# A decoder trunk on one core: an order planned with slack on VectorE and ScalarE, and three small steps on all partitions

## The chip, the cores and the metric

The kernel runs on one core of a Trainium2 chip. The core has five engines that run their own instruction queues side by side: TensorE (PE; its weight loads are shown as PEld), VectorE (DVE), ScalarE (ACT), GpSimd (POOL) and SyncE (SP), which here issues the transfers. The metric is the device time of one execution in microseconds (us). Times of a kernel are given as the median of several runs.

## The reference

The kernel computes a trunk of two layers on 256 tokens of width 1024, in float32. Cut to what matters:

```python
for l in range(DEPTH):                                   # 2
    h = _rms_norm(x, g_pre_mix[l])
    nq, kc, vc, ksel, vsel, kwin, vwin, gates, fq, fk, fv, ff = jnp.split(h @ w_in[l], ...)
    o_nsa = _nsa_mixer(...)     # 8 heads, 2 key/value groups: compressed, selected and window attention, gated
    o_fox = _fox_mixer(...)     # 8 heads
    mix = jnp.concatenate([o_nsa, o_fox], axis=-1) @ w_out[l]
    x = x + _rms_norm(mix, g_post_mix[l])
    h = _rms_norm(x, g_pre_mlp[l])
    y = jnp.square(jax.nn.relu(h @ w_up[l])) @ w_down[l]
    x = x + _rms_norm(y, g_post_mlp[l])
```

Two parts matter for the change. The compressed branch turns overlapping blocks of 32 keys (and values) into one key (value) each, by a small network with a bias at its end:

```python
hid = jax.nn.gelu(blocks @ w1 + b1)
return hid @ w2 + b2                                     # block keys, block values
```

The forgetting attention (`_fox_mixer`) adds differences of running sums of the log forget gates to its scores:

```python
log_f = jax.nn.log_sigmoid(f_logits + f_bias)
cum = jnp.cumsum(log_f, axis=1)
logits = q @ k.T * scale + cum[q] - cum[k]
```

## The kernel before

**Products.** Most matrix products run in TensorE's rounded float32 type. To keep float32 accuracy each operand is split in a rounded high part (`whi` for weights, written by ScalarE from the loaded chunk `wraw`) and a low part (`wlo`, VectorE: `wraw` minus `whi`), and three products are made: high by high, high by low, low by high. So every chunk of weights, 128 x 1024, needs one transfer, one ScalarE and one VectorE instruction. Transpositions are products with an identity (`cst`, `identr`).

**Stages of a layer.** Norm and input projections; rotation of queries and keys; the block network and the block keys and values; compressed, selected and window attention (NSA) and forgetting attention (FoX), whose score tiles `s` and `x` are exponentiated with VectorE and ScalarE (`pr`, row statistics `st`), transposed (`prT`, `prX`) and multiplied by the values into `o`; output projection of `oT`; MLP in eight chunks up and down. During attention, products of later projections (`acc<-xT,whi`, `acc<-whi,xT`, and behind them `x<-whi,oT`, `acc<-whi,oT`) are put between the attention's own products as fillers.

**What sets the order.** The program isn't emitted as it is written. A `Recorder` takes down every operation with its engine, a key for its rank, and a modelled duration (`op.cost = _cost(op, views)` in `add`). `schedule` then plays the program through as a list scheduler: on each engine it starts the ready operation that ranks first, with modelled costs, fixed latencies between engines (`_latency`) and the counts of free buffers; a load is taken to have ended 2900 ns after its bytes are through. `deadlines` derives due times from the order so found, `order` repeats this up to four times (PASSES) and keeps the plan that ends first. `emit` issues all in that order (this is the line L397 which most instructions of the profile carry). So a change of a modelled cost moves instructions of all engines, in the entire program. The cost of a VectorE instruction is

```python
return 68 + 64 * aps + n * (0.52 if fast else 1.04) + 10 * (op.name == "tensor_tensor_reduce")
```

in ns, with `n` columns and `aps` operands that are one value per partition; ScalarE's is `n / 1.2` plus 55 or 92, plus 93 for each such operand. The number of partitions doesn't enter.

**The three steps that are edited.** A tile has 128 partitions.
- `compressed_k` writes block keys into `kbd`, block-diagonal over two halves of 64 partitions: two VectorE instructions on 64 partitions each add the bias to the product's result; the other blocks stay zero from a memset at the program's start.
- `compressed_v` does the same for block values: one instruction on 128 partitions writes `vt` (result plus bias), then for each half of the partitions one copies it rounded into `vrep` (high part) and one subtracts (low part). `compressed_vT` transposes `vrep` on TensorE (tile `s<-identr,vrep`).
- `forget_sums` makes the running sums by two products into `s`. ScalarE copies them rounded into `cum`, in two pieces (128 and 256 columns); on partitions 32 to 63 and 96 to 127 VectorE replaces the copy by the low part, result minus copy, with two instructions for each of these two quarters. Products with `selr` add them to the scores (`s<-cum,selr`).

They are called once per layer, `compressed_k` directly and the others from a dictionary of steps that run beside the attention heads.

Of the kernel before, what the change touches and what calls it, by code (L numbers as in the profile page):

```python
# [18 lines left out]
F32 = mybir.dt.float32  # L19
F32R = mybir.dt.float32r  # L20
AF = mybir.ActivationFunctionType
# [3 lines left out]
P = 128  # L25
# [9 lines left out]
LANE = 0.9  # L35
PASSES = 4
LANDING = 2500.0
WAIT = 0.7
WARM = 4
ENTER, LEAVE = 90, 200  # L40
# [12 lines left out]
SEGS = ((0, 128, 0), (128, 384, 1))  # L53
GELU_C = 1.5957691216057308

C_ID, C_ROPE, C_SID, C_TRI, C_MASK, C_CM, C_M01, C_SEL, C_END = np.cumsum(
    [0, 128, 64, 32, 256, 256, 32, 32, 16]).tolist()


def constants():  # L60
    c = np.zeros((P, C_END), np.float32)
    i = np.arange(P)
    c[:, C_ID:C_ID + P] = np.eye(P)
    causal = np.where(i[None, :] <= i[:, None], 0.0, NEG)
    c[:, C_MASK + 128:C_MASK + 256] = causal
    c[:, C_TRI:C_TRI + 128] = i[:, None] <= i[None, :]
    c[:, C_TRI + 128:C_TRI + 256] = 1.0
    inv = np.float32(500000.0) ** (-np.arange(8, dtype=np.float32) * np.float32(2.0) / np.float32(16.0))
    for t in range(NT):
        ang = (i + t * P).astype(np.float32)[:, None] * inv[None, :].astype(np.float32)  # L70
        o = C_ROPE + 32 * t
        c[:, o:o + 8] = c[:, o + 8:o + 16] = np.cos(ang)
        c[:, o + 16:o + 24] = -np.sin(ang)
        c[:, o + 24:o + 32] = np.sin(ang)
        ok = (16 * np.arange(16) + 31)[None, :] <= (i + t * P)[:, None]
        c[:, C_CM + 16 * t:C_CM + 16 * t + 16] = np.where(ok, 0.0, NEG)
        c[:, C_M01 + 16 * t:C_M01 + 16 * t + 16] = ok
    for h in range(8):
        c[h::32, C_SEL + h] = 1.0
    for m in range(32):  # L80
        c[m::32, C_SID + m] = 1.0
    return c
# [88 lines left out]
class Recorder:  # L171
# [21 lines left out]
    def add(self, engine, name, args, kw):  # L193
        if self.group is not None:
            assert engine == "tensor"
            self.group.append((name, args, kw))
            return
        op = Op()
        op.engine, op.name, op.args, op.kw = engine, name, args, kw
        op.key = len(self.ops) if self.key is None else self.key  # L200
        if self.lane is not None and self.key is None:
            op.key = self.lane + LANE * (len(self.ops) - self.lane)
        op.urgent = self.hot
        views = []
        for _, a, k in args[2] if name == "stretch" else [(name, args, kw)]:
            views += [(i == 0, v) for i, v in enumerate(a) if isinstance(v, View)]
            views += [(i in ("out", "accum_out"), v) for i, v in k.items() if isinstance(v, View)]
        op.tile = _tile(op) if engine == "tensor" else None
        op.cost = _cost(op, views)
        deps = {} if self.after is None else {self.after: -1e9}  # L210
        op.bufs = []
        for is_out, v in sorted(views, key=lambda x: x[0]):
            b, m = v.buf, v.mask()
            if b not in op.bufs:
                op.bufs.append(b)

            def against(entries):
                for o, p, q, bank in entries:
                    if o is not op and o not in deps and (
                            (bank and engine == "tensor") or  # L220
                            (p[0] < v.p[1] and v.p[0] < p[1] and (m & q).any())):
                        deps[o] = _latency(o, op)

            against(b.writes)
            entry = (op, v.p, m, is_out and b.psum and engine == "tensor")
            if is_out:
                against(b.reads)
                b.writes = [w for w in b.writes if not (
                    w[0] in deps and v.p[0] <= w[1][0] and w[1][1] <= v.p[1] and not (w[2] & ~m).any())]
                b.writes.append(entry)  # L230
            else:
                if b.psum:
                    for o, _, _, _ in b.reads:
                        if o.engine != engine and o is not op and o not in deps:
                            deps[o] = 130.0
                b.reads.append(entry)
        op.deps = deps
        for b in op.bufs:
            if not b.ops:
                self.fifo.setdefault(b.tag, []).append(b)  # L240
            b.ops += 1
        op.succs = []
        for d in deps:
            d.succs.append(op)
        self.ops.append(op)
# [44 lines left out]
    def schedule(self):  # L290
# [41 lines left out]
        while events:  # L332
# [5 lines left out]
            for e, ops in waiting.items():  # L338
                while busy[e] <= t:
# [21 lines left out]
                    if e == "sync":  # L361
                        busy[e] = t + 450
                        bus = max(bus, t + 1150) + best.cost
                        best.end = bus + 2900
                    else:
                        busy[e] = best.end = t + best.cost
                        if e == "tensor" and best.tile != tiled:
                            busy[e] = best.end = best.end + (tiled == (P, P)) * ENTER + (tiled != (P, P)) * LEAVE
                            tiled = best.tile
# [69 lines left out]
def _cost(op, views):  # L439

    out = op.args[0] if op.args else op.kw["out"]
    n = int(np.prod(out.shape[1:]))
    if op.engine == "sync":
        v = views[0][1]
        return v.shape[0] * int(np.prod(v.shape[1:])) * 4 / 360.0
    if op.engine == "tensor":
        if op.name == "stretch":
            side = P // min(op.tile)
            return sum(_product(*x[:2], side) for x in op.args[2][::side])
        return _product(op.name, op.args, 1)  # L450
    if op.engine == "vector":
        if op.name == "reciprocal":
            return 60 + 6.5 * n
        if op.name == "tensor_reduce":
            n = int(np.prod(op.args[1].shape[1:]))
        fast = op.name in ("tensor_copy", "tensor_scalar", "memset") and not any(v.buf.psum for _, v in views)
        aps = sum(isinstance(v, View) for v in op.args[2:4]) if op.name == "tensor_scalar" else int(
            op.name == "scalar_tensor_tensor" and isinstance(op.args[2], View))
        return 68 + 64 * aps + n * (0.52 if fast else 1.04) + 10 * (op.name == "tensor_tensor_reduce")
    src = op.args[1]  # L460
    aps = sum(isinstance(op.kw.get(k), View) for k in ("bias", "scale", "accum_out"))
    return n / 1.2 + (55 if src.buf.psum else 92) + 93 * aps
# [52 lines left out]
def trunk(nc, A, consts_in, out, sbp, pp):  # L515
# [107 lines left out]
    nc.vector.memset(one_t, 1.0)  # L623
    kst = {}
    kbd = tile([P, 2, 2, 16], F32, name="kbd")
    nc.vector.memset(kbd, 0.0)
    vrep = tile([P, 2, 4, 2, 16], F32R, name="vrep")
    nc.vector.memset(vrep.bitcast(F32), 0.0)
    for s in "kv":
        kst[s] = tile([P, 16, 2, 16], F32, name="kst" + s)  # L630
    lf = [tile([P, 4, 32], F32, name=f"lf{t}") for t in range(NT)]
# [146 lines left out]
    for l in range(DEPTH):  # L778
# [140 lines left out]
        def hidden_gelu(s):  # L919
# [4 lines left out]
            nc.vector.tensor_mul(h, u, z)  # L924
            T["gh" + s] = h

        def compressed_k():
            ps = psum("s")
            for c in range(2):
                nc.tensor.matmul(ps[:, 0:32], par["w2"]["k"][:, c].rearrange("p j d -> p (j d)"), T["ghk"][:, c, :],  # L930
                                 start=c == 0, stop=c == 1)
            for j in range(2):
                hh = slice(j * HD, j * HD + HD)
                nc.vector.tensor_scalar(kbd[hh, :, j, :], ps[hh, 0:32].rearrange("p (g n) -> p g n", g=2),
                                        par["smT"][hh, 36:37], None, op0=OP.add)

        def compressed_v():

# [2 lines left out]
            for c in range(2):  # L941
                nc.tensor.matmul(ps[:, 0:32], par["w2"]["v"][:, c].rearrange("p j d -> p (j d)"), T["ghv"][:, c, :],
                                 start=c == 0, stop=c == 1)
            vt = small([P, 2, 16], "vt", 1)
            nc.vector.tensor_scalar(vt, ps[:, 0:32].rearrange("p (g n) -> p g n", g=2), par["smT"][:, 37:38], None,
                                    op0=OP.add)
            for j in range(2):
                hh = slice(j * HD, j * HD + HD)
                x = vt[hh, :, None, :].to_broadcast([HD, 2, 2, 16])
                nc.vector.tensor_copy(vrep[hh, :, 0:2, j, :], x)  # L950
                nc.vector.tensor_sub(vrep[hh, :, 2:4, j, :], x, vrep[hh, :, 0:2, j, :].bitcast(F32))

        def compressed_vT():
            ps = psum("s")
# [57 lines left out]
        def forget_sums():  # L1012
# [4 lines left out]
            nc.tensor.matmul(ps[:, :S], f[0], cst[:, C_TRI:C_TRI + S], start=True, stop=False)  # L1017
            nc.tensor.matmul(ps[:, P:S], f[1], cst[:, C_TRI:C_TRI + P], start=False, stop=True)
            cum = tile([P, 384], F32R, name="cum", tag="cum")
            for o, n in ((0, P), (P, S)):  # L1020
                nc.scalar.activation(cum[:, o:o + n], ps[:, :n], AF.Copy)
            for r in (slice(32, 64), slice(96, 128)):
                for o, n in ((0, P), (P, S)):
                    nc.vector.tensor_sub(cum[r, o:o + n], ps[r, :n], cum[r, o:o + n].bitcast(F32))
            T["cum"] = cum


# [520 lines left out]
```

## Time and profile before

| | us |
|---|---|
| median of 3 runs | 627.24 (627.1 to 627.25) |
| the profiled execution | 627.13 |
| its span, first to last instruction | 625.3 |
| TensorE busy | 616.8 |
| VectorE busy | 477.9 (1053 instructions) |
| ScalarE busy | 375.8 (728 instructions) |
| GpSimd busy | 0.2 |

The profiled execution lies 0.11 us under the median, and 1.8 us of its time are outside the span. The granted TensorE clock is 0.998 of full speed on average. Layer 0 runs to about 310 us, layer 1 after that; the attention of layer 0 lies at about 48 to 125 us, that of layer 1 at about 356 to 433 us.

How to read the lines shown below. A page line of busy time gives microseconds, the share of the span, and the number of instructions. A row of a timeline is: start in us, duration in us, engine, line, operation, output <- inputs by the program's names, shape, and how many of a kind follow each other; in brackets, idle time of the engine before it and what ended it. A group's row has the total busy time, the mean duration in ns of one, and the idle time before them. Products are pipelined: the next one starts before the last one has ended, so distances of starts tell more than durations.

### The profile page before, as it was taken

Reading aid. Unit: us, or ns where it says so; the run is one execution under the profiler, and the core shown is the slowest. Engines: PE = TensorE matmul, PEld = TensorE weight load, DVE = VectorE, ACT = ScalarE, POOL = GpSimd, SP = SyncE. Lnnn points to the kernel's source line nnn. Section 1 sums busy time; section 2 is a strip of 40 time slices with the busy share of each in tenths; the row PEclk is TensorE's granted clock in tenths of the full one; section 3 lists DMA queues with packets and bytes.
Section 4 is the critical chain, followed back from the end, with each engine's and each line's share of the span. In section 5 each row is a group of like instructions: output and inputs, shape, how many; then the busy total and the mean of one; then the engine's idle time right before and its main releaser. Section 6 shows DMA issues by size and latency. Waiting matters only on the chain.

```text
span 625.3 us, 9919 instructions
## 1 busy us (share of the span) xinstructions
PE 616.8 (99%) x3572; PEld 517.7 (83%) x3572; DVE 477.9 (76%) x1053; ACT 375.8 (60%) x728; POOL 0.2 (0%) x4
## 2 busy tenths in 40 slices
PE   9999999999999999999999999999999999999995
PEld 7988977788888888888888988777888888888884
DVE  6889998879966566567698899976996666566544
ACT  7768776567655455555476766764766555455432
POOL 0000000000000000000000000000000000000000
PEclk9999999999999999999999999999999999999999
DMA  8988555319666666654348682622386556666001
GB/s 324 404 310 285 199 161 157 91 64 320 221 200 202 187 183 203 193 178 128 117 129 273 231 313 67 226 85 95 123 306 187 191 179 198 197 179 202 24 1 67
DMA packets 33600, 115.69 MB, mean 185 GB/s; under 512 B 3984, under 2 KB 4112, under 8 KB 33552
## 3 DMA queue, kind: packets, MB, share of 16 engines
q1 hardware_dynamic: 33552, 115.07, 56.5%
q8 instruction: 28, 0.46, 0.3%
q14 instruction: 20, 0.16, 0.1%
HBM read 114.00 MB, written 1.05 MB: 184 GB/s over the span
## 4 chain that ended last, share of the span: by engine, by line
PE 87%; DVE 10%; issue 1%; DMA 1%; ACT 0%; DVEq 0%; SPq 0%
PE s L397 33%; PE acc L397 25%; PE x L397 24%; PE o L397 6%; DVE wlo L397 3%; DVE pr L397 3%; DMA first<-in_first_dram 1%; DVE gz L397 1%; DVE cs L397 0%; DVE fqT L397 0%; DVE prT L397 0%; DVE st L397 0%; DVE prX L397 0%; ACT whi L397 0%; DVE vrep L397 0%
## 5 line engine op out<-in xcount | busy, mean ns | idle before, releaser
L397 DVE TENSOR_TENSOR wlo<-wraw,whi 128x1024 fp32r<-128x1024 f32 (+1 forms) x188 | 225.4, 1203 | 85.1 <-ACT whi L397 81.9
L397 ACT ACTIVATE whi<-wraw 128x1024 fp32r<-128x1024 f32 (+1 forms) x188 | 195.2, 1042 | 111.8 <-PE acc L397 64.6
L397 PE MATMUL s<-xT,whi 128*128 128x512 f32 x448 | 112.0, 392 | 0.0
L397 PEld LDWEIGHTS s<-xT,whi 128*128 128x128 f32 x448 | 81.4, 189 | 15.2
L397 PE MATMUL acc<-whi,aT 128*128 128x512 f32 x256 | 88.6, 390 | 0.0
L397 PE MATMUL x<-whi,aT 128*128 128x512 f32 x256 | 88.4, 390 | 0.0
L397 PEld LDWEIGHTS s<-xT,wlo 128*128 128x128 f32 x448 | 61.1, 190 | 4.4
L397 PE MATMUL s<-xT,wlo 128*128 128x256 f32 x448 | 62.5, 282 | 0.0
L397 ACT ACTIVATE pr<-pr,st 128x256 f32<-128x256 f32 (+1 forms) x96 | 43.2, 452 | 24.8 <-DVE st L397 21.9
L397 PEld LDWEIGHTS acc<-whi,aT 128*128 128x128 f32 x256 | 48.1, 188 | 9.9
L397 PEld LDWEIGHTS x<-whi,aT 128*128 128x128 f32 x256 | 48.1, 188 | 9.7
L397 PE MATMUL acc<-wlo,aT 128*128 128x512 f32 x128 | 50.0, 390 | 0.0
L397 PE MATMUL x<-wlo,aT 128*128 128x512 f32 x128 | 50.0, 390 | 0.0
L397 PE MATMUL acc<-xT,whi 128*128 128x256 f32 x256 | 49.8, 286 | 0.0
L397 PEld LDWEIGHTS acc<-xT,whi 128*128 128x128 f32 x256 | 40.6, 190 | 1.6 <-ACT whi L397 0.4
L397 ACT ACTIVATE rl<-h 128x512 f32<-128x512 f32 x28 | 17.7, 633 | 35.8 <-DVE h L397 35.8
L397 PE MATMUL x<-whi,xT 128*128 128x512 f32 x112 | 37.1, 403 | 0.1
L397 PE MATMUL acc<-xT,wlo 128*128 128x256 f32 x128 | 36.4, 284 | 0.0
L397 PE MATMUL acc<-whi,xT 128*128 128x512 f32 (+1 forms) x128 | 36.3, 356 | 0.0
L397 DVE TENSOR_TENSOR h<-rl 128x512 f32<-128x512 f32 x28 | 19.4, 692 | 16.8 <-ACT rl L397 16.8
L397 ACT ACTIVATE rl<-x 128x512 f32<-128x512 f32 x24 | 14.8, 617 | 24.5 <-PE x L397 18.7
L397 PEld LDWEIGHTS acc<-wlo,aT 128*128 128x128 f32 x128 | 24.0, 188 | 4.9
(222 smaller groups left out, 975.4 us busy)
## 6 DMA issues: line engine op xcount, KB each, us to landing
wraw<-in_w_up_dram SPq DMA_DIRECT2D x64, 512.0 KB, 3.7
wraw<-in_w_down_dram SPq DMA_DIRECT2D x64, 512.0 KB, 3.5
wraw<-in_w_in_dram SPq DMA_DIRECT2D x36, 512.0 KB, 4.9
wraw<-in_w_out_dram SPq DMA_DIRECT2D x16, 512.0 KB, 5.6
w<-in_cmp_w_k_dram SPq DMA_DIRECT2D x8, 512.0 KB, 6.0
w<-in_cmp_w_v_dram SPq DMA_DIRECT2D x8, 512.0 KB, 5.8
first<-in_first_dram SPq DMA_DIRECT2D x7, 384.0 KB, 6.0
wraw<-in_w_in_dram SPq DMA_DIRECT2D x8, 288.0 KB, 4.3
```

Source lines behind the costliest of these rows:

```text
L397: getattr(getattr(self.nc, op.engine), name)(*[real(v) for v in args], **{k: real(v) for k, v in kw.items()})
```

## The change

1. `Recorder.add` adds 20 ns to the modelled cost of each VectorE and ScalarE operation (SLACK).
2. The cost model adds 100 ns for a VectorE operation on fewer than 128 partitions (`part`).
3. The modelled landing of a load is written as 900 + LATE with LATE = 2000; the sum is 2900 as before.
4. Block keys and block values: `by_half` writes both halves by two instructions on all 128 partitions, one for each group, as (result + bias) times a column of ones or zeros (`C_HALF`, two new constant columns). The memsets of `kbd` and `vrep` go.
5. Block values: `vrep`'s high part is one copy on ScalarE (before: two on VectorE), the low part one VectorE subtraction (before: two).
6. Forget sums: ScalarE writes the rounded copy (256 columns) and, scaled by a column of zeros and ones (`C_REST`), the unrounded one (256 columns), into a new tile `two`; VectorE makes `cum` by two instructions on 128 partitions (128 and 256 columns), copy times plus or minus one, plus the rest.

By 1 and 2, the order of the instructions changes on all engines over the whole program; the products themselves are the same. Per layer, block values and forget sums take VectorE 5 instructions where they took 9; the block keys' two stay two.

```diff
+SLACK, LATE = {"vector": 20, "scalar": 20}, 2000
...
+    for j in range(2):
+        c[j * HD:j * HD + HD, C_HALF + j] = 1.0
+
+    c[:, C_REST] = i // 32 % 2
+    c[:, C_REST + 1] = 1 - i // 32 % 2 * 2
...
-        op.cost = _cost(op, views)
+        op.cost = _cost(op, views) + SLACK.get(engine, 0)
...
-                        best.end = bus + 2900
+                        best.end = bus + 900 + LATE
...
+    part = 100 * (out.shape[0] < P)
...
-        return 68 + 64 * aps + n * (0.52 if fast else 1.04) + 10 * (op.name == "tensor_tensor_reduce")
+        return 68 + part + 64 * aps + n * (0.52 if fast else 1.04) + 10 * (op.name == "tensor_tensor_reduce")
...
-    nc.vector.memset(kbd, 0.0)
...
-    nc.vector.memset(vrep.bitcast(F32), 0.0)
...
+        def by_half(dst, ps, bias):
+
+            for g in range(2):
+                nc.vector.scalar_tensor_tensor(dst[:, g], ps[:, None, 16 * g:16 * g + 16].to_broadcast([P, 2, 16]),
+                                               par["smT"][:, bias:bias + 1],
+                                               cst[:, C_HALF:C_HALF + 2, None].to_broadcast([P, 2, 16]), op0=OP.add, op1=OP.mult)
+
         def compressed_k():
...
-            for j in range(2):
-                hh = slice(j * HD, j * HD + HD)
-                nc.vector.tensor_scalar(kbd[hh, :, j, :], ps[hh, 0:32].rearrange("p (g n) -> p g n", g=2),
-                                        par["smT"][hh, 36:37], None, op0=OP.add)
+            by_half(kbd, ps, 36)
...
         def compressed_v():
...
-            vt = small([P, 2, 16], "vt", 1)
-            nc.vector.tensor_scalar(vt, ps[:, 0:32].rearrange("p (g n) -> p g n", g=2), par["smT"][:, 37:38], None,
-                                    op0=OP.add)
-            for j in range(2):
-                hh = slice(j * HD, j * HD + HD)
-                x = vt[hh, :, None, :].to_broadcast([HD, 2, 2, 16])
-                nc.vector.tensor_copy(vrep[hh, :, 0:2, j, :], x)
-                nc.vector.tensor_sub(vrep[hh, :, 2:4, j, :], x, vrep[hh, :, 0:2, j, :].bitcast(F32))
+            vt = small([P, 2, 2, 16], "vt", 1)
+            by_half(vt, ps, 37)
+            x = vt.rearrange("p g j n -> p g (j n)")[:, :, None, :].to_broadcast([P, 2, 2, 32])
+            hi, lo = (vrep[:, :, b:b + 2].rearrange("p g a j n -> p g a (j n)") for b in (0, 2))
+            nc.scalar.activation(hi, x, AF.Copy)
+            nc.vector.tensor_sub(lo, x, hi.bitcast(F32))
...
             cum = tile([P, 384], F32R, name="cum", tag="cum")
+            two = tile([P, 2, S], F32R, name="two", tag="rl", bufs=2)
+            hi, rest = two[:, 0], two[:, 1].bitcast(F32)
+            nc.scalar.activation(hi, ps[:, :S], AF.Copy)
+            nc.scalar.activation(rest, ps[:, :S], AF.Copy, scale=cst[:, C_REST:C_REST + 1])
             for o, n in ((0, P), (P, S)):
-                nc.scalar.activation(cum[:, o:o + n], ps[:, :n], AF.Copy)
-            for r in (slice(32, 64), slice(96, 128)):
-                for o, n in ((0, P), (P, S)):
-                    nc.vector.tensor_sub(cum[r, o:o + n], ps[r, :n], cum[r, o:o + n].bitcast(F32))
+                nc.vector.scalar_tensor_tensor(cum[:, o:o + n], hi[:, :n].bitcast(F32), cst[:, C_REST + 1:C_REST + 2],
+                                               rest[:, :n], op0=OP.mult, op1=OP.add)
```

More of the change, by code (lines that the diff above doesn't have):

```diff
@@ L54 @@
 GELU_C = 1.5957691216057308
-C_ID, C_ROPE, C_SID, C_TRI, C_MASK, C_CM, C_M01, C_SEL, C_END = np.cumsum(
-    [0, 128, 64, 32, 256, 256, 32, 32, 16]).tolist()
+C_ID, C_ROPE, C_SID, C_TRI, C_MASK, C_CM, C_M01, C_SEL, C_HALF, C_REST, C_END = np.cumsum(
+    [0, 128, 64, 32, 256, 256, 32, 32, 8, 2, 2]).tolist()
 def constants():
```

## The prediction

> **What bounds the kernel now.** I read the page first (busy time, then the chain), then busy time by stretch, then TensorE's waits, and last the timelines of TensorE and VectorE where those waits lie.
>
> ```profile
> span 625.3 us, 9919 instructions
> PE 616.8 (99%) x3572; PEld 517.7 (83%) x3572; DVE 477.9 (76%) x1053; ACT 375.8 (60%) x728; POOL 0.2 (0%) x4
> PE 87%; DVE 10%; issue 1%; DMA 1%; ACT 0%; DVEq 0%; SPq 0%
> ```
>
> TensorE is busy 99% of the span, so its products set the time, and neither program has other products than the other. But a pipelined product that is held back counts as busy, and VectorE has 10% of the chain. Where? The columns of the next view are the stretch, its length, and the busy time of PE, PEld, DVE, ACT and POOL (with instructions), the clock, the DMA share and GB/s.
>
> ```profile
> 48.00:104.00 56.00, 55.78 (x430) 46.16 (x429) 55.57 (x198) 41.99 (x118) 0.00 (x0) 1.00 0.61 202
> 104.00:125.00 21.00, 21.00 (x131) 15.80 (x130) 16.07 (x48) 11.52 (x29) 0.00 (x0) 1.00 0.36 103
> 356.00:412.00 56.00, 55.50 (x429) 45.84 (x428) 55.54 (x199) 39.47 (x114) 0.00 (x0) 1.00 0.57 189
> ```
>
> In the attention of each layer VectorE is busy for 55.57 and 55.54 of 56 us: there two engines are full at once, while ScalarE has 14 to 16 us to spare. From 104 us on VectorE has 5 of 21 us free again, and the clock is 1.00 throughout. So only these two stretches can give something, and only as much as TensorE stands still in them. Its waits:
>
> ```profile
> PE s L397 <- DVE vrep L397: 0.4, 2, 0.2
> PE s L397 <- DVE st L397: 0.3, 1, 0.3
> ```
>
> That is 0.7 us, but idle time begins only when the pipeline has drained. The stall itself is the distance of two starts less what the products between them normally take:
>
> ```profile
> 63.94 0.30 PE L397 MATMUL s<-cst,pr 128*128 128x128 f32 x1
> 64.08 0.71 PE L397 MATMUL s<-identr,pcs 128*128 128x128 f32 x6
> ...
> 73.07 0.40 PE L397 MATMUL acc<-xT,whi 128*128 128x256 f32 x2
> 73.31 0.28 PE L397 MATMUL acc<-xT,wlo 128*128 128x256 f32 x1
> 73.43 0.40 PE L397 MATMUL acc<-xT,whi 128*128 128x256 f32 x2
> 74.02 0.33 PE L397 MATMUL s<-identr,vrep 128*128 128x128 f32 x2 [0.19 <-DVE vrep L397]
> ...
> 83.37 1.29 PE L397 MATMUL s<-cst,pr 128*128 128x128 f32 x6
> 84.42 0.71 PE L397 MATMUL x<-kx,qS 128*128 128x512 f32 x2
> 84.97 0.63 PE L397 MATMUL acc<-whi,xT 128*128 128x512 f32 x2
> 85.63 0.50 PE L397 MATMUL s<-kx,qS 128*128 128x256 f32 x2
> ...
> 380.98 0.28 PE L397 MATMUL acc<-xT,whi 128*128 128x256 f32 x1
> 381.43 0.34 PE L397 MATMUL s<-identr,vrep 128*128 128x128 f32 x2 [0.16 <-DVE vrep L397]
> ...
> 391.32 0.39 PE L397 MATMUL acc<-wlo,xT 128*128 128x512 f32 x1
> 392.04 0.50 PE L397 MATMUL s<-kx,qS 128*128 128x256 f32 x2 [0.34 <-DVE st L397]
> ```
>
> A 128x256 product takes 0.12 us (73.07 to 73.31, two of them), a 128x512 one twice that, about 0.235. So: 74.02 - 73.43 - 0.24 = 0.35. Six transpositions take 1.05 us (83.37 to 84.42) where 6 x 0.109 = 0.65 would do: 0.40. 85.63 - 84.97 - 0.47 = 0.19. In layer 1: 381.43 - 380.98 - 0.12 = 0.33, and 392.04 - 391.32 - 0.235 = 0.49. These five are 1.76 us. Eight gaps of 0.05 to 0.15 us, read the same way from the first at 63.94 (about 0.1) to the last behind 392.04, I put at 0.8. **TensorE loses about 2.6 us to a late VectorE**, 1.3 in each layer. The rest of the 625.3 us is products, the start and the tail.
>
> **The change, part by part.** What the edited instructions cost VectorE is the distance from their start to that of the next one:
>
> ```profile
> 51.42 1.22 DVE L397 TENSOR_TENSOR wlo<-wraw,whi 128x1024 fp32r<-128x1024 f32 x1
> 52.55 0.51 DVE L397 TENSOR_SCALAR kbd<-s,w 64x32 f32<-64x32 f32 x2
> 53.09 0.29 DVE L397 CUSTOM_DVE_ANT_0 pr<-s,cst 128x128 f32<-128x128 f32 x1
> ...
> 72.00 0.28 DVE L397 TENSOR_SCALAR vt<-s,w 128x32 f32<-128x32 f32 x1
> 72.16 0.31 DVE L397 CUSTOM_DVE_ANT_0 pr<-s,cst 128x128 f32<-128x128 f32 x1
> ...
> 72.37 0.42 DVE L397 CAST vrep<-vt 64x64 fp32r<-64x64 f32 x2
> 72.81 0.56 DVE L397 COPY prX<-s 128x384 f32<-128x384 f32 x1
> 73.40 0.47 DVE L397 TENSOR_TENSOR vrep<-vt,vrep 64x64 fp32r<-64x64 f32 x2
> 73.90 0.43 DVE L397 CUSTOM_DVE_ANT_0 pr<-x,cst 128x256 f32<-128x256 f32 x1
> ...
> 78.69 1.47 DVE L397 TENSOR_TENSOR cum<-s,cum 32x256 fp32r<-32x256 f32 x4
> 80.17 0.56 DVE L397 COPY prX<-s 128x384 f32<-128x384 f32 x1
> ```
> ```profile
> L397 DVE SCALAR_TENSOR_TENSOR mg<-mg,rsqrt,xo 128x256 f32<-128x256 f32 x24 | 10.0, 481 | 0.2
> L397 DVE TENSOR_TENSOR q<-rope,rope 128x128 f32<-128x128 f32 x4 | 1.1, 286 | 0.0
> ```
>
> Full-width instructions overlap: kbd starts at 52.55 while wlo runs to 52.64, 0.09 us earlier. Those on part of the partitions don't: the vrep pairs end at 72.79 and 73.87, the four cum at 80.16, and their followers start 0.01 to 0.03 us later. So the edit saves overlap as well as count.
> - Block keys (kbd): two halves, 53.09 - 52.55 = 0.54 us, become two full instructions of 128x32 at 0.16 each (vt, 72.00 to 72.16): 0.32. Saved 0.22.
> - Block values: vt 0.16, copies 72.81 - 72.37 = 0.44, subtractions 73.90 - 73.40 = 0.50, together 1.10. After: two of 128x32 (0.32) and one 128x128 subtraction (286 ns less 0.09: 0.20), together 0.52. Saved 0.58. The copy goes to ScalarE, 0.2 us of its 14 spare.
> - Forget sums: 80.17 - 78.69 = 1.48 us become one of 128x256 (481 ns less 0.09: 0.39) and one of 128x128, which I interpolate between that and the 0.16 of 32 columns: 0.26. Saved 0.83. ScalarE gets 128 columns more, 0.1 to 0.2 us.
> - Sum: 1.63 us of VectorE per layer. The one-operand forms could cost from 0.24 (a half kbd) to 0.48 (mg) each without overlap; at the dear end the saving is 0.9.
> - The memsets of kbd and vrep go, under the first load: 0. The constants' transfer loses 4 of 592 columns: 0. The load landing is 900 + 2000, as 2900 before: 0.
>
> By the Trainium skill, VectorE: DVE Perf Modes, section "The DRAIN you can't avoid", the next operation does not start until the pipe is empty; the saving would then be the durations alone, an estimate of 0.9 us per layer, and 0.1 us of lateness would stay in each. Its section "Two Vector instructions with no wait between them" has an instruction held only where its starting quadrant differs from the last one's; with kbd 0.09 us before wlo's end and the halves behind theirs, the trace agrees with the second.
>
> **The order.** The 20 ns per instruction exist only in the planner: 198 instructions x 20 ns = 4 us more of planned VectorE time in each 56 us stretch, so it must place consumers later. The printed order of the changed kernel shows this: the products are the same, moved against each other, with fillers (projection products) in front of consumers. I added the trace's start-to-start times along both printed orders from the stretch's first block-bias instruction, on each engine for itself. Before, VectorE's line falls 1.0 us (layer 0) and 1.1 us (layer 1) behind TensorE's unstalled line, and 23 and 21 of 64 waits come out late: that is the 1.3 us above, from another side. After, no wait is late; the smallest margin is 0.8 us in layer 0 and 0.6 in layer 1. At the vrep transpositions of layer 0 it goes from -0.4 to +0.9 (TensorE there 0.74 later, VectorE 0.59 earlier), at the scores of 85.63 from -1.0 to +1.3. Of the 1.3 us per layer I therefore take all; at worst half.
>
> Where it gets tighter: fillers used earlier are missing at the end of attention.
>
> ```profile
> 118.23 1.52 PE L397 MATMUL o<-prT,fV 128*64 128x256 f32 x16
> 119.68 0.50 PE L397 MATMUL acc<-whi,oT 128*128 128x512 f32 x1
> ```
> ```profile
> 120.43 0.69 DVE L397 TENSOR_TENSOR oT<-o,oT 128x512 fp32r<-128x512 f32 x1 [0.43 <-ACT oT L397]
> ```
>
> Behind the last forgetting-attention stretch (ends 119.68) twelve products, 2.8 us, stand before the first that reads its result oT; after, five, 1.14 us. oT's low half ends at 121.12, 1.44 us after 119.68; by the order the margin is 0.05 us, and a weight's low part (wlo, 1.13 us start to start) now stands ahead of it on VectorE, with its ScalarE copy ahead of that. I take 0.05 us per layer; the bounds are 0 and, with that wlo late, 1.1.
>
> SyncE's queue loads the halves of x ahead of one weight chunk at the start; the chunk's first use in the order lies 0.9 us behind its estimated landing: 0. Tail and MLP keep their order: 0.
>
> Sum on the profiled execution: its own time is 627.13 (span 625.3 and 1.8 around it), 0.11 under the median of 627.24. 627.13 - 2.6 + 0.1 = 624.6; against the median **624.7 us**.
>
> **Rivals.**
> - Half the gain. The vrep chain is now VectorE, ScalarE, VectorE, and a 1.06 us whi of ScalarE may stand before its copy; the planner's false costs may park instructions behind others that aren't ready. For it: ScalarE is 39 to 42 of 56 us busy. Against: between vt and the subtraction the order has 1.8 us of other VectorE work. Half of 2.6 returns: 626.0, from 625.5 to 627.2 as more comes back.
> - Slower: the end of attention. If the wlo ahead of oT comes late, TensorE stands still in both layers with nothing left to fill. It decides from 1.3 us per layer, where the gain is used up; wlo and the rest of oT make up to 1.13 + 0.69 = 1.8 per layer, so 624.7 + 3.6 = 628.3, and if also half the gain is missing, 629.6. For it: the margin of 0.05. Against: VectorE has 5 us free in 104 to 125, so wlo should have run before.
> - More gain. Other small stalls before the stretches (transpositions of q, 0.6 us in all) vanish, and two small-tile stretches that now adjoin save a mode switch of up to 0.3 each: 623.5. By the Trainium skill, TensorEngine Tiling (Array Packing), changing the tiling mode drains TensorE, which would leave the switch between two shapes as dear as before; no row before has the pair.
> - No effect: the padded plan ends as before and only VectorE's instructions shrink. Then the saved 1.6 us per layer still exceeds the lateness of 1.0 to 1.1, so most of the gain would come all the same; a forecast of 627.2 needs VectorE not to matter, against its 55.6 of 56.
>
> **How the numbers follow.** No change can be told within 0.2%, 1.25 us: faster is under 625.99, slower over 628.49. Forecast (623.9 to 625.9): 0.62. More gain: 0.07. Half the gain: 0.17, of which a third lies under 625.99. No effect: 0.03. Slower: 0.11, a fifth of it within the bound. Faster 0.62 + 0.07 + 0.05 = 0.74; same 0.12 + 0.03 + 0.02 = 0.17; slower 0.09. The range of 8 in 10 is 623.3 to 627.2; the likeliest case has 623.9 to 625.9.
>
> **What the profile after would show.** Right: VectorE about 1043 instructions and 474 us busy, with idle time appearing inside both stretches (some 54 of 56); TensorE about 614 busy; no waits on vrep or st; the cum group two instructions of under 0.5 us, overlapping. Wrong, if a wait of TensorE on oT appears at the end of attention, if VectorE waits for ScalarE's vrep or whi between 48 and 104, if the new forms take over 0.48 us, or if a stretch still has VectorE full.

## The result, and the profile after

The changed kernel takes 624.19 us (median of 6 runs, 623.63 to 624.30), the kernel before 627.24 (median of 6 here, 627.10 to 627.63): a ratio of 0.9949, 95% interval 0.9936 to 0.9962. The forecast was 624.7 in a range from 623.3 to 627.2. The profiled execution took 624.15 us, 622.3 of them in the span.

The page of the changed kernel (span; busy time of each engine; the chain that ended last):

```profile
span 622.3 us, 9920 instructions
PE 614.5 (99%) x3572; PEld 518.5 (83%) x3572; DVE 476.0 (76%) x1043; ACT 376.0 (60%) x730; POOL 0.2 (0%) x4
PE 98%; DVE 1%; issue 0%; DVEq 0%; ACT 0%
```

TensorE has 2.3 us less of busy time with the same products, so at least part of what counted as busy before was products held back, and VectorE's share of the chain went from 10% to 1%. Busy time in the two attention stretches (layer 1 now starts 2 us earlier):

```profile
48.00:104.00 56.00, 55.85 (x439) 47.30 (x437) 54.40 (x195) 41.19 (x115) 0.00 (x0) 1.00 0.61 209
354.00:410.00 56.00, 56.00 (x439) 47.23 (x438) 54.04 (x195) 40.53 (x116) 0.00 (x0) 1.00 0.53 189
```

VectorE has 1.6 and 2.0 us free where it had 0.4 and 0.5, and TensorE gets through 9 and 10 products more in the same 56 us. Of TensorE's waits for other engines one is left, at the start; those for vrep and st are gone:

```profile
PE o L404 <- DVE warm L404: 1.2, 1, 1.2
```

The new forms on VectorE, in its timeline:

```profile
53.11 0.41 DVE L404 SCALAR_TENSOR_TENSOR kbd<-s,w,cst 128x32 f32<-128x32 f32 x2
53.44 0.28 DVE L404 CUSTOM_DVE_ANT_0 pr<-s,cst 128x128 f32<-128x128 f32 x1
...
72.34 0.41 DVE L404 SCALAR_TENSOR_TENSOR vt<-s,w,cst 128x32 f32<-128x32 f32 x2
72.70 0.29 DVE L404 CUSTOM_DVE_ANT_0 pr<-s,cst 128x128 f32<-128x128 f32 x1
72.92 0.08 DVE L404 DVE_READ_ACCUMULATOR2_ANT st<- 128x1 f32 x1
72.92 0.55 DVE L404 COPY prX<-s 128x384 f32<-128x384 f32 x1
73.39 1.32 DVE L404 TENSOR_TENSOR fkT<-acc,rT 128x512 f32<-128x512 f32 x2
74.63 0.28 DVE L404 TENSOR_TENSOR vrep<-vt,vrep 128x128 fp32r<-128x128 f32 x1
74.83 0.66 DVE L404 TENSOR_SCALAR pr<-pr,st,gate 128x128 f32<-128x128 f32 x2
...
81.10 0.48 DVE L404 SCALAR_TENSOR_TENSOR cum<-two,cst 128x256 fp32r<-128x256 f32 x1
81.50 0.16 DVE L404 RECIPROCAL st<-st 128x2 f32<-128x2 f32 x1
81.57 0.34 DVE L404 SCALAR_TENSOR_TENSOR cum<-two,cst 128x128 fp32r<-128x128 f32 x1
81.82 0.67 DVE L404 TENSOR_SCALAR pr<-pr,st,gate 128x128 f32<-128x128 f32 x2
```

From start to next start, in layer 0: block keys 0.33 us, block values 0.36 + 0.20, forget sums 0.40 + 0.25, together 1.54 against 0.54 + 1.10 + 1.48 = 3.12 before. The saving is 1.58, forecast 1.63.

One new stall stands in TensorE's timeline, right where VectorE writes fkT:

```profile
73.70 0.28 PE L404 MATMUL acc<-xT,wlo 128*128 128x256 f32 x1
74.13 0.50 PE L404 MATMUL acc<-whi,xT 128*128 128x512 f32 x1
```

0.43 us where a 128x256 product takes 0.12: 0.31 lost, and 0.10 behind the next product. The product starts a new sum in one of the two buffers acc; the first fkT instruction (73.39, done at 74.07) still reads one of them, and the product starts 0.06 us behind its end.

To compare kernels I take TensorE's time apart in the same way over a whole profile: distance of each start to the next, less the distance that the same product has between neighbours of the same kind (the value that a quarter of all such distances, over all kernels, stay under). What is left over is counted as a stall; 1.35 us of it in the two attentions, in small pieces, is in every kernel and holds no gap above 0.06. The rest is the products' own time. "Projections" are the stretches ahead of each attention. The split depends on how finely neighbours are told apart: with other groupings the fall from before to changed is 2.3 to 2.8 us in the attention and 0.5 to 0.1 in the products.

| kernel | median us | stalls: start | projections | attention | products |
|---|---|---|---|---|---|
| before | 627.24 | 0.75 | 1.28 | 4.27 | 609.3 |
| changed (slack 20, edits, price) | 624.19 | 1.15 | 0.77 | 1.82 | 608.9 |
| slack alone | 625.68 | 0.67 | 0.78 | 3.61 | 608.8 |
| price alone | 625.25 | 1.35 | 1.42 | 2.41 | 609.3 |
| edits alone | 624.79 | 0.96 | 1.27 | 1.53 | 609.2 |
| edits and price | 624.37 | 0.96 | 1.08 | 1.35 | 609.2 |
| edits and price, seven instructions mispriced | 626.30 | 0.93 | 1.03 | 3.34 | 609.3 |
| changed, slack 10 | 623.72 | 1.01 | 0.83 | 1.95 | 608.5 |
| changed, slack 40 | 625.11 | 0.63 | 1.20 | 2.13 | 608.4 |

The kernel before has 2.9 us of stalls in the attention above the common 1.35 (forecast: 2.6), the changed one 0.5. The stalls are those of the profiled execution, the times are medians; with the price alone the profiled execution was the slowest, 626.03. The start differs between profiles from 0.6 to 1.35, in no relation to the edits; so differences of a few tenths between medians are not read as effects.

### The profile page after: what moved, and what is told of

Read it like the earlier page. It is cut to its first block, busy times and chain, and to the rows that moved or that the text cites. A ratio compares the mean times of both kernels' runs of the same rounds, so it can differ in the third digit from the quotient of the medians.

```text
span 622.3 us, 9920 instructions
## 1 busy us (share of the span) xinstructions
PE 614.5 (99%) x3572; PEld 518.5 (83%) x3572; DVE 476.0 (76%) x1043; ACT 376.0 (60%) x730; POOL 0.2 (0%) x4
## 4 chain that ended last, share of the span: by engine, by line
PE 98%; DVE 1%; issue 0%; DVEq 0%; ACT 0%
PE s L404 35%; PE acc L404 31%; PE x L404 25%; PE o L404 7%; DVE x L404 0%; DVE m L404 0%; DVEq L1554 0%; DVE fkT L404 0%; DVE rsqrt L404 0%; DVE prX L404 0%; DVE vt L404 0%; DVE warm L404 0%; DVE pr L404 0%; ACT rl L404 0%; DVEq L404 0%
```

## The experiments

Each was timed over 5 rounds beside the kernel before, which had medians from 627.21 to 627.36. "Price" is the 100 ns in the planner for VectorE instructions on fewer than 128 partitions.

### Which of the three parts brings the gain?

Between prediction and experiments I set the planner's formula beside the trace of before. It had the halves of kbd at 2 x 165 ns (the trace: 0.54 us), vrep's copies at 2 x 101 (0.44) and subtractions at 2 x 135 (0.50), and the four cum at 2 x (334 + 201) (1.48): short by 0.21 + 0.24 + 0.23 + 0.41 = 1.09 us per layer. Instructions on all partitions agree with it much better: 1133 ns planned for wlo, which the trace shows at 1.13 us from start to start.

**Slack alone**: the kernel before with

```diff
-        op.cost = _cost(op, views)
+        op.cost = _cost(op, views) + SLACK.get(engine, 0)
```

> The kernel before with 20 ns more modelled cost on every VectorE and ScalarE instruction; none of the three steps edited, no price for partial partitions. Three theories. Plan: VectorE is late before because the plan's prices for the ten instructions on part of the partitions are too low (in the trace the kbd, vrep and cum instructions take 1.09 us more per layer than their modelled 68 ns plus columns; the others agree with the model within about 1%), and a plan with enough slack puts the consumers behind the true time: 624.6, from 624.0 to 625.4. Work: only less work on VectorE helps, since it is busy 55.6 of 56 us: 626.6 to 627.6. Slack: the padding is what helps: 624.6 as well.

Measured: 625.68 us, ratio 0.9974 (0.9963 to 0.9984). TensorE in its timeline:

```profile
73.22 0.28 PE L398 MATMUL acc<-xT,wlo 128*128 128x256 f32 x1
74.21 0.50 PE L398 MATMUL acc<-whi,xT 128*128 128x512 f32 x1 [0.71 <-DVE fkT L398]
```

It gains 1.5 us, about half of the whole, and outside the range given. The stalls in the attention hardly fall (3.61 against 4.27), since this one of 0.87 takes the place of the one at vrep; by the table the gain is 0.5 in the projections and 0.5 in the products, of which the last is uncertain by the 0.3 or so that the grouping moves. A padding that is the same for every instruction does not fully mend a price that is wrong for ten of them.

**Price alone**: the kernel before with

```diff
+    part = 100 * (out.shape[0] < P)
...
-        return 68 + 64 * aps
+        return 68 + part + 64 * aps
```

> The kernel before with only the 100 ns in the modelled cost of VectorE instructions on fewer than 128 partitions; VectorE's work is that of before. Plan: the modelled time now fits the trace (ten instructions, 1.0 us per layer, against 1.09 measured), so the lateness goes though no work is saved and nothing is padded: 624.8, from 624.2 to 625.6, VectorE still about 55.5 busy in the 56 us. Work: 626.6 to 627.6. Slack: 626.6 to 627.6.

Measured: 625.25 us, ratio 0.9968 (0.9955 to 0.9980). Its page's busy times, and the two stretches:

```profile
PE 616.5 (99%) x3572; PEld 518.4 (83%) x3572; DVE 477.8 (77%) x1053; ACT 375.5 (60%) x728; POOL 0.2 (0%) x4
```
```profile
48.00:104.00 56.00, 56.00 (x437) 47.03 (x436) 55.49 (x202) 42.61 (x119) 0.00 (x0) 1.00 0.63 206
354.00:410.00 56.00, 56.00 (x441) 47.03 (x441) 55.68 (x203) 41.01 (x118) 0.00 (x0) 1.00 0.58 190
```

VectorE has the 1053 instructions of before and is as full as before, and still 2.0 of 3.05 us are gained: TensorE's lost time in the attention falls from 4.27 to 2.41. So most of the gain does not need a VectorE with less to do; it needs a plan that does not believe VectorE faster than it is. The other 0.9 us, down to the 624.37 of the same price with the edits, come back with the work saved (see the next experiment).

**Edits alone**, and **edits with the price**: the changed kernel with

```diff
-SLACK, LATE = {"vector": 20, "scalar": 20}, 2000
+SLACK, LATE = {"vector": 0, "scalar": 0}, 2000
```

and, for the edits alone, `part = 0 *` in place of `part = 100 *`.

> The changed kernel with slack 0 and no price for partial partitions: only the three steps on all partitions. Plan: the under-priced instructions are gone, the model is true: 624.8, from 624.2 to 625.6. Work: 1.6 us per layer saved, 624.8 as well. Slack: 626.6 to 627.6.

> The changed kernel with slack 0: three steps on all partitions, and the price for the few instructions on part of the partitions that are left (copies of key and value blocks ahead of the attention). Plan and work: as the edits alone, within 0.5 us of it, 624.2 to 625.6; what it is slower than the changed kernel (624.2) is what the 20 ns are worth beside the edits. Slack: 626.6 to 627.6.

Measured: 624.79 us, ratio 0.9959 (0.9947 to 0.9972), and 624.37 us, ratio 0.9952 (0.9939 to 0.9964). The stretches of the second:

```profile
48.00:104.00 56.00, 56.00 (x439) 47.24 (x438) 55.59 (x199) 42.71 (x119) 0.00 (x0) 1.00 0.63 213
354.00:410.00 56.00, 56.00 (x439) 47.12 (x438) 54.71 (x197) 40.70 (x117) 0.00 (x0) 1.00 0.61 196
```

Without any slack VectorE is nearly as full as before, and TensorE has no gap above 0.06 us in the attention. The edits bring most of the gain, 2.4 us; the 20 ns add 0.2 to edits and price, too little for these intervals to tell from nothing.

### Is it the price, or the work?

The edits take away work and wrong prices at once. So, with the instructions of "edits and price" as they are, the planner was given prices that are too low again:

```diff
         op.cost = _cost(op, views) + SLACK.get(engine, 0)
+        if engine == "vector" and args and args[0].buf.name in ("kbd", "vt", "vrep", "cum") and name != "memset":
+            op.cost -= 155
```

> The edits with the price for partial partitions and slack 0 (624.37 us), but the modelled cost of the seven VectorE instructions that write kbd, vt, vrep and cum is lowered by 155 ns each, 1.09 us per layer, as much as the plan before was short by. The instructions themselves are the same. Plan: TensorE is held up again by about 1 us per layer, at vrep and at the scores behind it: 626.3, from 625.5 to 627.0. Work: the work is as small as in the edits, 624.4, at most 624.8.

Measured: 626.30 us (11 runs), ratio 0.9987 (0.9978 to 0.9996). The waits of TensorE, and its timeline in layer 1:

```profile
PE s L406 <- DVE vrep L406: 0.4, 2, 0.2
```
```profile
380.57 0.28 PE L406 MATMUL acc<-xT,whi 128*128 128x256 f32 x1
381.08 0.35 PE L406 MATMUL s<-identr,vrep 128*128 128x128 f32 x2 [0.23 <-DVE vrep L406]
```

These are the rows of the kernel before again, at the same place, with 381.08 - 380.57 - 0.12 = 0.39 lost. The stalls in the attention rise from 1.35 to 3.34, 2.0 us for 2 x 1.09 us of false price, and the time by 1.9. With the work saved, a plan that is short by what the first plan was short by gives back 1.9 of the 2.9 us.

Four of these kernels make a table of price and work (medians in us):

| | prices too low | prices near the trace |
|---|---|---|
| work of before | 627.24 | 625.25 |
| work saved by the edits | 626.30 | 624.37 |

The price is worth 2.0 and 1.9 us, whatever the work; the work saved is worth 0.9 us, whatever the price. The false price is the larger cause, at about two thirds, and VectorE's work the smaller. The smaller one is less sure: with the false price its interval is 0.25 to 1.4 us, and a plan that is only reshuffled moves by a few tenths too (see the slack below).

### What does the slack do beside that?

The changed kernel with slack on one engine, with 10 or 40, and with the slack only outside or inside the attention's list of operations:

```diff
-SLACK, LATE = {"vector": 20, "scalar": 20}, 2000
+SLACK, LATE = {"vector": 20, "scalar": 0}, 2000
```
```diff
-SLACK, LATE = {"vector": 20, "scalar": 20}, 2000
+SLACK, LATE = {"vector": 0, "scalar": 20}, 2000
```
```diff
-SLACK, LATE = {"vector": 20, "scalar": 20}, 2000
+SLACK, LATE = {"vector": 40, "scalar": 40}, 2000
```
```diff
-SLACK, LATE = {"vector": 20, "scalar": 20}, 2000
+SLACK, LATE = {"vector": 10, "scalar": 10}, 2000
```

> The changed kernel with the 20 ns on VectorE only. The plan theory has VectorE's price as what counts: 624.2, within 0.4 of the changed kernel, with the stall behind fkT at about 74 us as there. If ScalarE's slack were what loosens the projections, 624.6 or more.

> The changed kernel with the 20 ns on ScalarE only. Plan theory: VectorE's price is true without padding, so no stall in the attention and none behind fkT: 624.3, from 623.9 to 624.8. If VectorE's slack is what takes the small stalls off the projections (0.55 and 0.77 us before, 0.39 and 0.41 after), those come back and it is 624.4 or more.

> The changed kernel with 40 ns in place of 20. VectorE's 198 instructions of a stretch are then planned 8 us too long, over what TensorE leaves room for. Plan theory: consumers placed ever later run out of fillers, and instructions are parked in wrong places: 624.9, from 624.2 to 626.5. Slack theory: more is better, 623.8 or less.

> The changed kernel with 10 ns in place of 20. Plan theory: the price is already true at 0 (624.37 with slack 0), so anything near it gives 624.0 to 624.8, without a trend; a trend from 0 over 10 to 20 and 40 (624.37, 624.19 and 625.11 for the other three) would have its best near 10 to 20: 624.2 or less.

For the last two the factor is `(self.lane is None)`, and `(self.lane is not None)` for the inside:

```diff
-        op.cost = _cost(op, views) + SLACK.get(engine, 0)
+        op.cost = _cost(op, views) + SLACK.get(engine, 0) * (self.lane is None)
```

> The changed kernel with the 20 ns on VectorE and ScalarE only for operations outside the attention's own list (projections, norms, MLP, weight splits asked for there). Beside the edits with true prices (624.37), the full slack takes about 0.3 us of small stalls off the projections and 0.4 off switches between kinds of products, and brings a stall of 0.4 behind fkT at 74 us. If the first two come from slack outside and the last from slack inside the attention, this is the best: 623.8, from 623.4 to 624.2. If what slack does is only to reshuffle the plan, it lies anywhere from 624.0 to 624.9.

> The changed kernel with the 20 ns only for the attention's own operations. The counterpart: stall behind fkT kept, no gain in the projections: 624.8, from 624.4 to 625.3. Only a reshuffle: anywhere from 624.0 to 624.9.

Measured: vector only 624.61 (ratio 0.9955, 0.9943 to 0.9968), scalar only 624.85 (0.9959, 0.9945 to 0.9973), slack 40 625.11 (0.9963, 0.9951 to 0.9976), slack 10 623.72 (0.9942, 0.9930 to 0.9955), outside only 624.47 (0.9955, 0.9941 to 0.9968), inside only 624.49 (0.9953, 0.9940 to 0.9965).

The expectation for the slack outside failed by 0.7 us. The stall behind fkT is gone there, as expected, but another stands at its place, with 73.34 - 72.80 - 0.12 = 0.42 us lost: TensorE waits for gh, the hidden values of the block network, which VectorE writes behind a wlo:

```profile
72.80 0.28 PE L404 MATMUL acc<-xT,wlo 128*128 128x256 f32 x1
73.34 0.49 PE L404 MATMUL s<-gh,w 128*128 128x32 f32 x3 [0.26 <-DVE gh L404]
```
```profile
71.85 1.21 DVE L404 TENSOR_TENSOR wlo<-wraw,whi 128x1024 fp32r<-128x1024 f32 x1
72.97 0.22 DVE L404 TENSOR_TENSOR gh<-gu,gz 128x64 f32<-128x64 f32 x1
```

A stall behind fkT, of 0.23 us or more, is in every kernel that pads inside the attention: in layer 0 with the vector's slack (0.26), with 10 and with 20, in layer 1 with the scalar's slack (0.23, where none was expected) and with the slack inside only, in both layers with 40 and with the slack alone. None of the four kernels with the edits and no slack there (edits alone, edits and price, mispriced, outside only) has one; price alone has a small one (0.18). So padding inside the attention goes with that stall, on either engine; which step of the planner places it so was not traced.

The times of vector only and scalar only lie just outside the ranges given (624.2 within 0.4, and 623.9 to 624.8). So does slack 10, and by more: 623.72 is under the plan theory's 624.0 to 624.8, and 624.37, 623.72, 624.19 and 625.11 for 0, 10, 20 and 40 are what the expectation named as a trend with its best near 10 to 20. One kernel for each value can't tell such a trend from chance. The six kernels of this section lie from 623.7 to 625.1, on both sides of the 624.37 without slack; none of their intervals excludes it. That slack does no more here than reshuffle the plan, by a few tenths either way, fits this and is not shown. Slack 10 has the lowest time of all, 0.47 under the changed kernel, with the runs of the two (623.53 to 624.00 and 623.63 to 624.30) overlapping; that it is the better kernel is likely, not shown.

With 40 the limit shows. Its stretches, and TensorE in the MLP of layer 1:

```profile
48.00:104.00 56.00, 55.93 (x436) 47.21 (x436) 52.05 (x189) 41.37 (x113) 0.00 (x0) 1.00 0.56 184
354.00:410.00 56.00, 55.92 (x424) 47.29 (x424) 51.94 (x190) 39.10 (x111) 0.00 (x0) 1.00 0.58 187
```
```profile
436.77 0.86 PE L404 MATMUL s<-cst,mg 128*128 128x128 f32 x5
437.88 0.50 PE L404 MATMUL s<-whi,xT 128*128 128x512 f32 x1 [0.24 <-ACT xT L404]
```

VectorE now stands idle for 4 of 56 us, in a plan made for slower engines, and the attention's stalls are not fewer (2.13). And a stall stands in a stage that had none: 437.88 - 436.77 - 5 x 0.11 = 0.56 us lost at the first products of the MLP. What the table's columns leave out of the profiled execution is 12.5 us with slack 40 and 11.5 with slack 20, so most of what slack 40 loses lies outside the attention. Why the plan came to be late there was not traced.

### What makes a half instruction dear?

Behind the last instruction of the changed kernel, 16 VectorE subtractions were added whose result nothing reads:

```diff
+            spans = [(0, 128, 128)] * 4 + [(0, 64, 126)] * 4 + [(64, 128, 124)] * 4 + [(0, 64, 122), (64, 128, 122)] * 2
+            for i, (lo, hi, n) in enumerate(spans):
+                self.nc.vector.tensor_sub(t[lo:hi, i * 128:i * 128 + n], src[lo:hi, 0:n], src[lo:hi, 128:128 + n])
```

> The changed kernel with 16 subtractions on VectorE appended behind its last instruction, without a wait between them, on a tile that nothing reads: four on 128 partitions (128 columns), four on partitions 0 to 63 (126), four on partitions 64 to 127 (124), and four that alternate between the halves (122). If an instruction on part of the partitions never overlaps its neighbour, the last three groups take about 0.30 us each and only the first 0.20. If it is the change of the start partition that holds an instruction back, as the Trainium skill's page VectorE: DVE Perf Modes has it in its section on two instructions with no wait between them, the second and third group take 0.20 each like the first, and only the alternating one 0.30.

Measured: 625.4 us in one run; the added instructions run for 3.77 us. Their groups (busy time of all four, mean ns of one, idle time before), and the four stretches, from the start of one group to the next, with VectorE's busy time:

```profile
L410 DVE TENSOR_TENSOR probe<-cst 64x122 f32<-64x122 f32 x4 | 1.1, 281 | 0.1
L410 DVE TENSOR_TENSOR probe<-cst 128x128 f32<-128x128 f32 x4 | 0.9, 284 | 0.0
L410 DVE TENSOR_TENSOR probe<-cst 64x124 f32<-64x124 f32 x4 | 0.9, 284 | 0.0
L410 DVE TENSOR_TENSOR probe<-cst 64x126 f32<-64x126 f32 x4 | 0.9, 275 | 0.0
```
```profile
618.89:619.69 0.80, 0.80 (x4) 1.00 0.64 238
619.70:620.58 0.88, 0.87 (x5) 0.50 0.97 365
620.59:621.48 0.89, 0.89 (x4) 0.50 0.01 2
621.49:622.66 1.17, 1.12 (x4) 0.50 0.00 0
```

All 16 last 275 to 290 ns, but the starts are 0.20 us apart in the groups that keep their start partition, on 128 partitions, on the lower half and on the upper half alike (the second and third stretch hold one change of 0.29 and 0.30 at their end), and 0.29 in the group that alternates. It is the change of the start partition that costs 0.09 us, not the number of partitions. This is what the Trainium skill, VectorE: DVE Perf Modes, section "Two Vector instructions with no wait between them", states: an instruction is held if its operands start in another quadrant than the last ones did.

## Why the prediction was right

- **What bounds it.** TensorE loses 2.6 us in the two attentions: measured 2.9 by the finer subtraction. That only these stretches could give something was too narrow: the projections gave 0.5 (1.28 to 0.77) and the products themselves 0.1 to 0.5, which is the case "more gain" that the prediction had left out of its sum.
- **The edits' cost.** 1.58 us saved per layer for 1.63 forecast. The reason given, that instructions on part of the partitions do not overlap, was wrong in its form: those that start on another partition than the one before don't. It made no difference to the sum here: in the trace of before none of these instructions overlaps its follower, which fits steps that alternate between halves or quarters.
- **The order.** That the 20 ns "must place consumers later" and so remove 1.3 us per layer is the step that failed. The sum came out because three causes were stacked of which one would have done most: slack alone leaves the attention's stalls at 3.61, edits alone at 1.53. In this part the good number is luck. The prediction gave VectorE's fullness as the reason; the larger one was ten instructions per layer that the plan took for 1.09 us shorter than they are, about the lateness of 1.0 to 1.1 us that the prediction had added up without seeing where it came from. Price alone gains 2.0 us with VectorE full, mispricing alone gives back 1.9; the work saved is worth 0.9. The argument against the rival "no effect", that the work saved exceeds the lateness of an order that stays as it was, was not tested: every kernel here with the edits has an order of its own.
- **The margins.** The prediction added up each engine's line for itself and found no wait late and at least 0.6 us of margin. In the run vrep's low part ended at 74.91 and its transpositions began at 75.16, a margin of 0.25 and not 0.9, and the buffer read by fkT was 0.4 late. VectorE had itself waited for TensorE before, which the separate sums leave out; the two longest such waits ahead of these margins, 0.20 and 0.43 us, come to about the 0.65 that is missing:

```profile
54.14 0.69 DVE L404 TENSOR_TENSOR fqT<-acc,rT 128x512 f32<-128x512 f32 x1 [0.20 <-PE acc L404]
...
65.11 0.42 DVE L404 CUSTOM_DVE_ANT_0 pr<-x,cst 128x256 f32<-128x256 f32 x1 [0.43 <-PE s L404]
```

- **The new wait.** The 0.1 us set aside for new stalls was to fall at the end of attention. It was 0.4, and at fkT. At the end of attention there was none; VectorE and TensorE there, after the changed kernel's last forgetting-attention stretch of layer 0:

```profile
119.66 1.23 DVE L404 TENSOR_TENSOR wlo<-wraw,whi 128x1024 fp32r<-128x1024 f32 x1 [0.36 <-ACT whi L404]
120.89 0.69 DVE L404 TENSOR_TENSOR oT<-o,oT 128x512 fp32r<-128x512 f32 x1
```
```profile
120.15 0.50 PE L404 MATMUL x<-wlo,oT 128*128 128x512 f32 x1
120.48 0.63 PE L404 MATMUL x<-whi,oT 128*128 128x512 f32 x2
```

  The wlo ahead of oT ends at 120.89, when ScalarE's half of oT has just been written, and costs nothing. The rival "slower" did not occur, but its wlo ran to the last moment, as the margin of 0.05 had it.
- **The sum.** Attention -2.45, projections -0.5, products -0.4, start +0.4 (which varies between profiles), small pieces elsewhere: -3.0 in the profiled executions, 627.13 to 624.15. The forecast of -2.6 + 0.1 = -2.5 meets the attention's -2.45, in which stalls of 2.9 became 0.5. The projections and products came on top, and the start took 0.4 back; neither stood in the forecast.

## What to carry to other kernels

Where an order is planned ahead, ask first whether the plan's prices agree with the trace: one microsecond of false price on seven instructions cost one microsecond per layer here, while the 1.6 us of work saved per layer on an engine that was 99% full in its stretch was worth about half of that. Padding every price was a poor substitute here: 20 ns on each instruction brought half of the gain, and 40 beside the edits left VectorE idle in the attention and TensorE waiting in the MLP. And margins along a new order hold only if the engines' lines are added up together, each waiting for the other.

## What was not expected of the hardware

On VectorE a run of instructions on the upper 64 partitions alone is as cheap as one on all 128, 0.20 us from start to start for 124 to 128 columns; each change between the halves costs 0.09 us, in the first instruction behind the change. The probe moved between partitions 0 and 64 only. Steps that must work on parts of the partitions could be sorted so that those with the same start partition follow each other; that was not tried in this kernel.
